# A hybrid encoder layer in float32: weight buffers of the first SwiGLU block, a raw pool, the place of a query projection, and a second bank for side work

## The chip, the cores and the metric

The kernel runs on one core of a Trainium2 chip, in one launch. A core has TensorE (matrix products; PE in the rows, PEld its weight loads), VectorE (DVE), ScalarE (ACT), GpSimd (POOL) and SyncE, whose queue (SP) issues all of this kernel's DMA transfers, in order. The metric is device microseconds of one execution; lower is better.

## The reference

One encoder layer is applied to two requests (1024 and 256 tokens, handled here as 1280 columns), model width 1024, all in float32:

```python
def encoder_layer(x, mem, ...):
    m = mixer(x, ...)              # differential attention | bidirectional RG-LRU, gated, then one projection
    x = layer_norm(ALPHA * x + m, ...)
    x = layer_norm(ALPHA * x + cross_attention(x, mem, ...), ...)   # 4 heads, 256 memory tokens
    x = layer_norm(ALPHA * x + swiglu(x, w_in, w_out), ...)         # 2816 hidden features
...
# in the mixer
proj = x @ w_in                    # q, k, v, x and y of the RG-LRU, two gates
attn_out = diff_attention(q, k, v, lam)     # 8 heads of 2 x 64; softmax - lam * softmax
merged = sigmoid(g_attn) * (attn_out @ p_attn) + sigmoid(g_lru) * (lru_out @ p_lru)
return merged @ w_mix_out
```

## The kernel before

Every float32 product is made of three float32r products: both operands are split into a high part (a copy) and a low part (value minus copy), and high x high, high x low and low x high are added in PSUM. A weight block of 128 x 1024 is loaded as `raw`, copied to `wh` (ScalarE in most stages, L187) and subtracted to `wl` (GpSimd or VectorE, L190) by `wload`. Its result lies in `WT`, four pairs of buffers that live through the whole kernel; `raw` lies in `RW`, two buffers, or in another pool that the caller names.

The stages, in order of time: input projections with the RG-LRU; attention; attention projection and gating (L961 to L963); mixing projection with layer norm; cross-attention; its output projection with layer norm; SwiGLU and the last layer norm, in two halves of 640 tokens.

*Attention.* A unit is a head and 128 query rows. `scores` writes `s` (two buffers of two banks), VectorE reduces (L743), ScalarE takes the exponential (L745), `probs` combines the two halves (L761) and transposes them (`t`, L767), and `values` multiplies (`o`, L785 to L787) and normalises with the tile `pm` (L794, L799). `t` and `pm` share the pool `ps_t`, of two banks. Between units TensorE gets side work from a generator, `fillers`: the memory's keys and values, the gates `sld` and `sad` (evicted with a tanh, L697) and `p_lru` (evicted by L705), each multiplication of 24 matmuls (L283, L286, L287) on the pool `ps_m`, of one bank. The tokens come in three chunks, and the last in the generator's order has columns 512 to 1023. The order of the program is not that of the engines: a scheduler orders each engine's instructions by a priority (the order of the program, and for fillers 120 places later) and by when it thinks that an instruction can start. A pool hands out its buffers in the order of the program, and each waits until the buffer's last holder is done.

*Cross-attention.* For each head `h` and chunk `c` the loop projects queries and then runs the units of the pair before (`prev`), 256 tokens each. `prepare` computes the seven sums of weights of SwiGLU blocks 0 to 3 and stores them in `fpd`.

*SwiGLU.* Each of 22 blocks of 128 hidden features is computed by Strassen's seven products (L355 to L357), each with its own weight of 128 x 512, high and low. `reloaded` fetches those of blocks 0 to 3 from `fpd`, in both halves: two of the seven in the buffers of `RW` (block 0) or in one pair of `WT` (blocks 1 to 3), five in the pool `ws`, whose five pairs each block uses up. `out_group` then multiplies with the output weights `wo` of a group of two blocks (L1202 to L1204), which `wload` puts in `WT`. `pair_ops` prepares the weights of the other blocks on the fly, with raw buffers of `RW` and of `rx`, four buffers.

Of the kernel before, what the change touches and what calls it, by code (L numbers as in the profile page):

```python
# [10 lines left out]
F32R = mybir.dt.float32r  # L11
I32 = mybir.dt.int32
AF = mybir.ActivationFunctionType
ALU = mybir.AluOpType
# [30 lines left out]
RELOAD = 4  # L45
# [83 lines left out]
E_FO = 'VG'  # L129
# [11 lines left out]
def encoder_layer_kernel(ctx: ExitStack, tc: tile.TileContext, i, y_out):  # L141
    nc = tc.nc
    V, S, G, PE, SP = nc.vector, nc.scalar, nc.gpsimd, nc.tensor, nc.sync

    EN = {"V": V, "S": S, "G": G}
# [7 lines left out]
    def f32(ap):  # L153
        return ap.bitcast(F32)
# [110 lines left out]
    WT = pool(ctx, "wt", 4)  # L265
    RW = pool(ctx, "raw", 2)

    def wload(src, heng, leng, wp=WT, rp=RW):
        raw = rp.tile([128, 1024], F32, tag="raw", name="raw")
        SP.dma_start(raw, src)  # L270
        h = wp.tile([128, 1024], F32R, tag="wh", name="wh")
        l = wp.tile([128, 1024], F32R, tag="wl", name="wl")
        split(h, l, raw, heng, leng)
        return h, l

    def gemm_fm(pp, w, op, evac, tag="mm", name="ps", after=None):
        wh, wl = w
        hs, ls, n = op
        ps = pp.tile([128, 512], F32, tag=tag, name=name)[:, :n]
        for k in range(8):  # L280
            a, b = (z[:, k * 128:k * 128 + 128] for z in (wh, wl))
            h, l = hs[k // 2][:, k % 2, :], ls[k // 2][:, k % 2, :]
            ins = PE.matmul(ps, a, h, start=(k == 0), stop=False)  # L283
            if after is not None and k == 0:
                tc.add_manual_dep(ins.ins, after.ins.name, ORDER, reason="order")
            PE.matmul(ps, a, l, start=False, stop=False)  # L286
            PE.matmul(ps, b, h, start=False, stop=(k == 7))  # L287
        evac(ps)
# [370 lines left out]
    with ExitStack() as es:  # L659
# [16 lines left out]
        def fillers():  # L676
            for j in range(16):
                w = wload(i["xa_wkv"][j], EN[E_FWH], EN[E_FWL])
                stage = st.tile([128, M], F32, tag="mst", name="mst", bufs=MSTB)
                gemm_fm(ps_m, w, mem, lambda ps: S.activation(stage, ps, AF.Copy, scale=0.0625 if j < 8 else 1.0), tag="m", after=anchor[0])  # L680
                if j < 8:
                    SP.dma_start(kxd[j], stage)
                else:
                    ps = ps_m.tile([128, 512], F32, tag="m", name="ps")
                    for t in range(4):
                        PE.transpose(ps[:, t * 128:t * 128 + 128], stage[:, t * 128:t * 128 + 128], ident)
                    vt = st.tile([128, 4, 128], F32, tag="mst", name="mvt", bufs=MSTB)
                    S.activation(vt, ps.rearrange("p (t e) -> p t e", e=128), AF.Copy)
                    SP.dma_start(vxd[:, (j - 8) * 128:(j - 7) * 128].rearrange("(t p) e -> p t e", p=128), vt)
                yield 5.3  # L690
            for c0, n in (CHUNKS[2], CHUNKS[0], CHUNKS[1]):
                x = stored(xd, c0, n)
                for dst, base in ((sld, 48), (sad, 40)):
                    for b in range(NB):
                        w = wload(i["w_in"][base + b], EN[E_FWH], EN[E_FWL])
                        g = st.tile([128, M], F32, tag="mst", name="th", bufs=MSTB)[:, :n]
                        gemm_fm(ps_m, w, x, lambda ps: S.activation(g, ps, AF.Tanh, scale=0.5), tag="m", after=anchor[0])  # L697
                        SP.dma_start(dst[b, :, c0:c0 + n], g)
                        yield 5.4 * n / 512
                lru = stored(lrud, c0, n)  # L700
                for b in range(NB):
                    w = wload(i["p_lru"][b], EN[E_FWH], EN[E_FWL])
                    g = st.tile([128, M], F32, tag="mst", name="g", bufs=MSTB)[:, :n]
                    SP.dma_start(g, sld[b, :, c0:c0 + n])
                    gemm_fm(ps_m, w, lru, lambda ps: V.scalar_tensor_tensor(g, g, 1.0, ps, ALU.add, ALU.mult), tag="m", after=anchor[0])  # L705
                    SP.dma_start(gd[b, :, c0:c0 + n], g)
                    yield 5.4 * n / 512

# [266 lines left out]
    with ExitStack() as es:  # L975
# [24 lines left out]
        with ExitStack() as es1:  # L1000
# [100 lines left out]
            prev = None  # L1101
            for h in range(4):
                for c in range(3):
                    now = h, c, queries(h, c)
                    if (h, c) in PREAT:
                        with tc.high_priority(offset=-PREP):
                            prepare(PREAT[h, c])
                    if prev is not None:
                        attends(*prev)
                    prev = now  # L1110
# [5 lines left out]
    with ExitStack() as es:  # L1116
# [44 lines left out]
        with ExitStack() as es1:  # L1161
# [6 lines left out]
            po = pool(es1, "psE", 2, PSUM)  # L1168

            def reloaded(f):  # L1170
                if f == 0:
                    gs = [RW.tile([128, 1024], F32, tag="raw", name="raw").bitcast(F32R) for t in "hl"]
                else:
                    gs = [WT.tile([128, 1024], F32R, tag="w" + t, name="w" + t) for t in "hl"]
                u = [tuple(ws.tile([128, 512], F32R, tag=t, name="s" + t) for t in "hl") for _ in range(5)]
                w = [tuple(g[:, c * 512:c * 512 + 512] for g in gs) for c in range(2)] + u
                for n, _ in P_ORDER:
                    for m in range(2):
                        SP.dma_start(f32(w[n][m]), fpd[f, n, m])
                return w  # L1180
# [30 lines left out]
            for half_ in range(2):  # L1211
                r0 = half_ * 640
                ys = []
                groups = [tuple(range(sum(GR[half_][:n]), sum(GR[half_][:n + 1]))) for n in range(len(GR[half_]))]
                for fs in groups:
                    hs_ = []
                    for f in fs:
                        hs_.append(hidden(f, *((E_M1, E_SL1) if f == NF - 1 else (E_M, E_SL))))
                        if pending:
                            z, t = pending.pop()  # L1220
                            xf = rx.tile([128, 8, 128], F32, tag="raw", name="xf")
                            feature_major(po, "o", z, xf)
                            save(xf, t - 5)
                    if not ys:
                        for t in range(5):
                            ys.append(yp.tile([128, D], F32, tag="z", name="y"))
                            SP.dma_start(ys[t], x2d[r0 + t * 128:r0 + t * 128 + 128, :])
                    wo = [wload(i["ffn_out"][f], EN[E_FO[0]], EN[E_FO[1]]) for f in fs]
                    last = None
                    if fs is groups[-1]:  # L1230
                        SP.dma_start(gt, i["ln3_g"].partition_broadcast(128))
                        SP.dma_start(bt, i["ln3_b"].partition_broadcast(128))
                        if half_ == 0:
                            operands()
                            for j in range(5):
                                xf = rx.tile([128, 8, 128], F32, tag="raw", name="xf")
                                SP.dma_start(xf, x2t[:, :, j * 128:j * 128 + 128].rearrange("k p t -> p k t"))
                                combine(j, xf, rx.tile([128, 4, 4, 64], F32, tag="raw", name="tt"))

                        def last(t):  # L1240
                            rows = slice(r0 + t * 128, r0 + t * 128 + 128)
                            end = half_ == 1 and t == 4
                            with tc.high_priority(offset=0 if half_ else -LNP):
                                power = layer_norm(st, ys[t], gt, bt, end, not (half_ and t >= 3))
                            if end:
                                for hs in (slice(0, 512), slice(512, 1024)):
                                    SP.dma_start(y_out[rows, hs], ys[t][:, hs])
                            if not half_ or t < 3:
                                with tc.high_priority(offset=0 if half_ else -LNP):
                                    G.tensor_tensor(ys[t], ys[t], bt, ALU.add)  # L1250
                            if not end:
                                with tc.high_priority(offset=0 if half_ else -LNP):
                                    SP.dma_start(y_out[rows, :], ys[t])

                    out_group(hs_, fs, wo, ys, fs[0] == 0, last)
# [65 lines left out]
```

## Time and profile before

| | |
|---|---|
| median of 3 runs | 2826.33 us (2823.35 to 2829.81) |
| the profiled execution | 2822.44 us, its span 2820.5 us |
| TensorE busy | 2739.3 us of the span |
| VectorE, ScalarE, GpSimd busy | 1705.5, 1138.6, 919.3 us |

Times in the trace count from the start of the span. A matmul's duration in it is longer than the step to the next one, since they are pipelined; only idle time between them is a wait.

### The profile page before, as it was taken

The page shows a single profiled execution, that of the slowest core. Times are in us where ns is not written, and L with a number is a line of the kernel's source. Part 1 is how long each engine was busy: PE and PEld are TensorE (multiplying, and loading weights), DVE is VectorE, ACT ScalarE, POOL GpSimd, SP SyncE. Part 2 cuts the span into 40 slices and gives each one's busy share as a digit, 9 for nine tenths or more (in the row PEclk, how much of TensorE's full clock was granted, in tenths as well). Part 3 has the DMA queues.
Part 4 walks back from the last instruction along what each step waited for, and adds up shares of the span by engine and source line. Part 5 has one row for each costly group of instructions (what it writes and reads, how often), then busy time and mean ns, then how long its engine had stood idle before and what let it go on. Part 6 is the DMA issues. An engine that isn't in the chain of part 4 may idle for free.

```text
span 2820.5 us, 40319 instructions
## 1 busy us (share of the span) xinstructions
PE 2739.3 (97%) x15240; PEld 2411.8 (86%) x15240; DVE 1705.5 (60%) x2517; ACT 1138.6 (40%) x1921; POOL 919.3 (33%) x576
## 2 busy tenths in 40 slices
PE   9999999999999999999999999998999998999998
PEld 7888888887889888888788889887999997899997
DVE  4545667415667755644345576563677777577776
ACT  3656444415666655455211144321223333233232
POOL 0000000013345543344100100052566559565555
PEclk9999999999999999999999999999999999999999
DMA  9633545565567756844887576658322225622221
GB/s 358 208 109 112 175 152 190 174 206 178 162 202 222 244 169 199 252 141 162 303 273 235 172 276 210 217 186 299 116 79 90 83 82 193 227 84 80 79 80 60
DMA packets 292450, 496.26 MB, mean 176 GB/s; under 512 B 22560, under 2 KB 165664, under 8 KB 292256
## 3 DMA queue, kind: packets, MB, share of 16 engines
q1 hardware_dynamic: 292256, 493.69, 53.6%
q8 instruction: 120, 1.97, 0.3%
q14 instruction: 74, 0.61, 0.1%
HBM read 342.08 MB, written 151.52 MB: 175 GB/s over the span
## 4 chain that ended last, share of the span: by engine, by line
PE 67%; DVE 11%; DMA 11%; issue 4%; ACT 4%; POOL 2%; SPq 1%; DVEq 0%; ACTq 0%; POOLq 0%
PE ps L283 4%; PE ps L286 4%; PE ps L287 4%; PE ps L357 3%; PE ps L355 3%; PE ps L356 3%; PE ps L520 3%; PE ps L521 3%; PE ps L522 3%; PE o L1202 3%; PE o L1203 3%; PE o L1204 2%; PE ps L885 2%; PE ps L883 2%; PE ps L884 2%
## 5 line engine op out<-in xcount | busy, mean ns | idle before, releaser
L190 POOL TENSOR_TENSOR wl<-raw,wh 128x1024 fp32r<-128x1024 f32 x132 | 321.3, 2435 | 973.5 <-ACT wh L187 863.6
L187 ACT ACTIVATE wh<-raw 128x1024 fp32r<-128x1024 f32 (+1 forms) x224 | 224.4, 1006 | 492.0 <-PE ps L286 155.2
L520 PE MATMUL ps<-xh,wh 128*128 128x512 f32 (+1 forms) x768 | 274.4, 357 | 12.1 <-ACT xh L187 5.9
L355 PE MATMUL ps<-xbh,sh 128*128 128x320 f32 x880 | 273.1, 310 | 8.9 <-DMA sh<-fpd 7.0
L521 PE MATMUL ps<-xl,wh 128*128 128x512 f32 (+1 forms) x768 | 273.9, 357 | 0.5 <-DVE xl L190 0.5
L357 PE MATMUL ps<-xbh,sl 128*128 128x320 f32 x880 | 272.6, 310 | 0.4 <-DMA sl<-fpd 0.3
L522 PE MATMUL ps<-xh,wl 128*128 128x512 f32 (+1 forms) x768 | 273.0, 356 | 0.0
L356 PE MATMUL ps<-xbl,sh 128*128 128x320 f32 x880 | 272.4, 310 | 0.0
L283 PE MATMUL ps<-fh,wh 128*128 128x512 f32 (+1 forms) x704 | 258.6, 367 | 11.7 <-DVE g L705 5.0
L286 PE MATMUL ps<-fl,wh 128*128 128x512 f32 (+1 forms) x704 | 255.7, 363 | 2.5 <-DMA fl<-memd 2.5
L287 PE MATMUL ps<-fh,wl 128*128 128x512 f32 (+1 forms) x704 | 255.1, 362 | 0.0
L190 DVE TENSOR_TENSOR wl<-raw,wh 128x1024 fp32r<-128x1024 f32 (+1 forms) x136 | 177.5, 1311 | 96.6 <-ACT wh L187 84.7
L743 DVE TENSOR_REDUCE nm<-s 128x1 f32<-128x1024 f32 (+1 forms) x160 | 167.3, 1059 | 93.8 <-PE s L742 93.4
L1205 DVE SCALAR_TENSOR_TENSOR y<-y,o 128x512 f32<-128x512 f32 x200 | 133.5, 681 | 115.4 <-PE o L1204 108.0
L850 POOL TENSOR_TENSOR rstd<-rstd,mhalf 128x1 f32<-128x1 f32 x30 | 34.5, 1152 | 498.4 <-DVE rstd L849 498.4
L1202 PE MATMUL o<-wh,hh 128*128 128x512 f32 x440 | 175.0, 398 | 11.8 <-DVE wh L189 4.3
L745 ACT ACTIVATE e<-s,nm 128x1024 f32<-128x1024 f32 (+1 forms) x160 | 158.6, 996 | 57.6 <-DVE nm L743 55.7
L355 PEld LDWEIGHTS ps<-xbh,sh 128*128 128x128 f32 x880 | 165.8, 188 | 12.8 <-DMA sh<-fpd 8.4
L520 PEld LDWEIGHTS ps<-xh,wh 128*128 128x128 f32 x768 | 146.3, 190 | 34.3 <-ACT xh L187 5.9
L1203 PE MATMUL o<-wl,hh 128*128 128x512 f32 x440 | 173.1, 394 | 0.0
L356 PEld LDWEIGHTS ps<-xbl,sh 128*128 128x128 f32 x880 | 165.9, 189 | 3.8
L357 PEld LDWEIGHTS ps<-xbh,sl 128*128 128x128 f32 x880 | 165.7, 188 | 3.4 <-DMA sl<-fpd 0.9
(261 smaller groups left out, 7241.6 us busy)
## 6 DMA issues: line engine op xcount, KB each, us to landing
raw<-w_in SPq DMA_DIRECT2D x80, 512.0 KB
raw<-ffn_in SPq DMA_DIRECT2D x80, 512.0 KB
raw<-ffn_out SPq DMA_DIRECT2D x44, 512.0 KB
q<-qd SPq DMA_DIRECT2D x320, 64.0 KB
raw<-p_lru SPq DMA_DIRECT2D x24, 512.0 KB
qd<-hl SPq DMA_DIRECT2D x16, 640.0 KB
kd<-hl SPq DMA_DIRECT2D x16, 640.0 KB
vd<-v SPq DMA_DIRECT2D x40, 256.0 KB
```

The source lines that it names most:

```text
L190: leng.tensor_tensor(l, src, f32(h), ALU.subtract)
L283: ins = PE.matmul(ps, a, h, start=(k == 0), stop=False)
L286: PE.matmul(ps, a, l, start=False, stop=False)
L287: PE.matmul(ps, b, h, start=False, stop=(k == 7))
L355: PE.matmul(ps, w[n][0][:, ks], xb[m][0][:, k, :], start=(k == 0), stop=False)
L356: PE.matmul(ps, w[n][0][:, ks], xb[m][1][:, k, :], start=False, stop=False)
L357: PE.matmul(ps, w[n][1][:, ks], xb[m][0][:, k, :], start=False, stop=(k == 3))
L520: PE.matmul(ps, wh[:, ks], h[:, k, :], start=(k == 0), stop=False)
L521: PE.matmul(ps, wh[:, ks], l[:, k, :], start=False, stop=False)
L522: PE.matmul(ps, wl[:, ks], h[:, k, :], start=False, stop=(k == 7))
L1202: PE.matmul(ps, hs_[a][0][:, ts], wo[a][0][:, hs], start=(a == 0), stop=False)
L1203: PE.matmul(ps, hs_[a][0][:, ts], wo[a][1][:, hs], start=False, stop=False)
```

## The change

Four edits. In the last chunk the p_lru multiplications of odd `b` take their bank from `ps_t`, the others from `ps_m` as before. In the cross-attention the last query projection, of (3, 2), is written behind the units of (3, 1). In the first half SwiGLU block 0 takes all seven weights from the four pairs of `WT`, and block 1 takes the two buffers of `RW`; the second half is as before. The output weights of blocks 0 to 3 are loaded through `rx` in place of `RW`.

```diff
                     w = wload(i["p_lru"][b], EN[E_FWH], EN[E_FWL])
...
-                    gemm_fm(ps_m, w, lru, lambda ps: V.scalar_tensor_tensor(g, g, 1.0, ps, ALU.add, ALU.mult), tag="m", after=anchor[0])
+                    last = c0 == 512 and b % 2
+                    gemm_fm(ps_t if last else ps_m, w, lru, lambda ps: V.scalar_tensor_tensor(g, g, 1.0, ps, ALU.add, ALU.mult), tag="t" if last else "m", after=anchor[0])
...
             for h in range(4):
                 for c in range(3):
+                    if (h, c) == (3, 2):
+                        attends(*prev)
+                        prev = None
                     now = h, c, queries(h, c)
...
             def reloaded(f):
-                if f == 0:
+                if f == 0 and not half_:
+                    z = [[WT.tile([128, 1024], F32R, tag="w" + t, name="w" + t) for t in "hl"] for _ in range(4)]
+                    w = [tuple(y[:, c:c + 512] for y in x) for x in z for c in (0, 512)][:7]
+                    for n, _ in P_ORDER:
+                        for m in range(2):
+                            SP.dma_start(f32(w[n][m]), fpd[f, n, m])
+                    return w
+                if f == 1 - half_:
                     gs = [RW.tile([128, 1024], F32, tag="raw", name="raw").bitcast(F32R) for t in "hl"]
...
-                    wo = [wload(i["ffn_out"][f], EN[E_FO[0]], EN[E_FO[1]]) for f in fs]
+                    wo = [wload(i["ffn_out"][f], EN[E_FO[0]], EN[E_FO[1]], rp=rx if f < RELOAD else RW) for f in fs]
```

What it makes of the order of the engines is shown at three places. Line numbers are those of each kernel (in the changed one they are one higher from L706 on, and up to eleven higher at the end).

The first is ScalarE where TensorE comes to the last chunk's first gates: `th` is the eviction of a filler, `wh` the copy of a filler's weight, `e` the exponential, `pth` and `pf` the copies of a transposition, `sq` and `ob` the end of a pair; the numbers tell the tiles apart. Before:

```order
L187 ACTIVATE wh_10600<-raw_10598 128x1024
L745 ACTIVATE e_12249,ss_12234<-s_12243,nm_12233 128x1024
L697 ACTIVATE th_10228<-ps_10229 128x512
L770 ACTIVATE pth_11904<-t_12018 128x4x128
L773 ACTIVATE pf_12024<-t_12018 128x512
L745 ACTIVATE e_12241,ss_12234<-s_12235,nm_12233 128x1024
L770 ACTIVATE pth_12125<-t_12135 128x4x128
L187 ACTIVATE wh_10731<-raw_10729 128x1024
L697 ACTIVATE th_10359<-ps_10360 128x512
L770 ACTIVATE pth_12127<-t_12142 128x4x128
```

And with the change:

```order
L790 ACTIVATE sq_12180<-o_12155 128x256
L792 ACTIVATE ob_12182<-o_12155,g08_84 128x256
L187 ACTIVATE wh_10600<-raw_10598 128x1024
L697 ACTIVATE th_10228<-ps_10229 128x512
L187 ACTIVATE wh_10731<-raw_10729 128x1024
L697 ACTIVATE th_10359<-ps_10360 128x512
L187 ACTIVATE wh_10810<-raw_10808 128x1024
L697 ACTIVATE th_10393<-ps_10394 128x512
L187 ACTIVATE wh_10923<-raw_10921 128x1024
L697 ACTIVATE th_10570<-ps_10571 128x512
```

Such pairs of a copy and an eviction follow each other 14 times, with nothing of the attention between; on TensorE 325 matmuls of fillers stand in one run there.

The second is TensorE where the attention ends and the attention projection (`ps<-fh,wh`, L961 before, L962 now) begins. Before, fillers stand between the last rows of the attention, and after these come 120 more matmuls of fillers (five multiplications) and then the projection:

```order
L794 MATMUL pm<-ones,sq 128x1 x2
L799 MATMUL pm<-ident,rs 128x128 x2
L283 MATMUL ps<-fh,wh 128x512
L286 MATMUL ps<-fl,wh 128x512
L287 MATMUL ps<-fh,wl 128x512
```

With the change the last filler stands 308 matmuls ahead of the projection, and all of these are the attention's; the last are:

```order
L768 MATMUL t<-ident,e 128x128 x2
L800 MATMUL pm<-ident,rs 128x128 x2
L795 MATMUL pm<-ones,sq 128x1 x2
L786 MATMUL o<-pth,vh 128x256
L787 MATMUL o<-ptl,vh 128x256
L788 MATMUL o<-pth,vl 128x256
...
L800 MATMUL pm<-ident,rs 128x128 x2
L795 MATMUL pm<-ones,sq 128x1 x2
L800 MATMUL pm<-ident,rs 128x128 x2
L962 MATMUL ps<-fh,wh 128x512 x8
```

The projection also begins with the first product of all eight blocks, where it began with one block.

The third is the queue SP between the halves of SwiGLU: `ffn_out` is an output weight, `y<-y` an output of the first half, `wh`, `wl`, `sh`, `sl` the reloaded weights of a block. Before:

```order
L327 DMA raw<-ffn_in 128x1024
L1253 DMA y<-y 128x1024
L1227 DMA y<-x2d 128x1024
L1179 DMA wl<-fpd 128x512
L1179 DMA wh<-fpd 128x512 x2
L1179 DMA wl<-fpd 128x512
L1253 DMA y<-y 128x1024 x2
L1179 DMA sh<-fpd 128x512
L1179 DMA sl<-fpd 128x512
L1231 DMA lng<-ln_g 128x1024
L1227 DMA y<-x2d 128x1024
L270 DMA raw<-ffn_out 128x1024 x2
```

And with the change:

```order
L270 DMA raw<-ffn_out 128x1024 x3
L1264 DMA y<-y 128x1024
L270 DMA raw<-ffn_out 128x1024
L1238 DMA y<-x2d 128x1024
L1264 DMA y<-y 128x1024
L1190 DMA wh<-fpd 128x512
L1190 DMA wl<-fpd 128x512
L1190 DMA wh<-fpd 128x512
```

The four output weights of blocks 0 to 3 stand ahead of the outputs and of the reloaded weights now; two of them stood behind three outputs.

## Rows read from the trace of the kernel before

**Rows 1.** The page's part 1: busy time, share of the span, instructions.

```profile
PE 2739.3 (97%) x15240; PEld 2411.8 (86%) x15240; DVE 1705.5 (60%) x2517; ACT 1138.6 (40%) x1921; POOL 919.3 (33%) x576
```

**Rows 2.** Windows: length, busy per engine (instructions), granted TensorE clock, DMA share, GB/s.

```profile
1193.60:1393.90 200.30, 193.23 (x1016) 162.99 (x1016) 95.75 (x150) 94.36 (x173) 71.32 (x43) 0.99 0.58 193
1781.40:1813.40 32.00, 25.40 (x190) 24.11 (x189) 23.20 (x41) 18.46 (x41) 0.00 (x0) 0.91 0.94 315
1807.30:1814.30 7.00, 4.88 (x22) 4.40 (x21) 3.37 (x4) 2.12 (x4) 0.00 (x0) 0.52 1.16 330
1929.70:1957.00 27.30, 18.81 (x117) 17.67 (x116) 10.78 (x19) 5.70 (x9) 3.24 (x3) 0.87 0.96 343
1937.00:1944.00 7.00, 2.80 (x10) 2.80 (x11) 0.69 (x1) 0.51 (x1) 0.00 (x0) 0.52 0.95 343
2370.00:2417.00 47.00, 37.42 (x220) 33.94 (x218) 23.74 (x37) 8.38 (x11) 29.56 (x17) 0.93 0.87 319
2394.50:2401.50 7.00, 4.94 (x15) 4.07 (x16) 4.04 (x4) 0.00 (x0) 5.45 (x3) 0.51 1.04 413
1387.50:1391.00 3.50, 3.50 (x10) 2.76 (x9) 1.17 (x1) 0.72 (x1) 0.00 (x0) 0.53 0.83 270
```

**Rows 3.** Waits of TensorE, 1184 to 1394: total us, times, longest.

```profile
PE ps L283 <- DVE g L705: 4.5, 5, 2.1
```

**Rows 4.** Timeline near the side work's end: start, duration, [idle before <-releaser].

```profile
1376.47 0.39 PE L283 MATMUL ps<-fh,wh 128*128 128x512 f32 x1
...
1377.15 0.39 PE L283 MATMUL ps<-fh,wh 128*128 128x512 f32 x1
...
1384.77 1.22 DVE L190 TENSOR_TENSOR wl<-raw,wh 128x1024 fp32r<-128x1024 f32 x1 [2.10 <-ACT wh L187]
1385.91 0.68 DVE L705 SCALAR_TENSOR_TENSOR g<-g,ps 128x512 f32<-128x512 f32 x1
...
1386.74 0.47 PE L283 MATMUL ps<-fh,wh 128*128 128x512 f32 x1 [2.15 <-DVE g L705]
```

**Rows 5.** Waits of TensorE, 1781 to 1960.

```profile
PE ps L355 <- DMA sh<-fpd: 5.8, 1, 5.8
PE o L1068 <- DVE ob L190: 5.3, 3, 2.1
PE t L932 <- DVE z L858: 1.4, 1, 1.4
...
PE s L1045 <- ACT e L1053: 1.1, 1, 1.1
```

**Rows 6.** Waits of TensorE, 2368 to 2420.

```profile
PE o L1202 <- DVE wh L189: 4.3, 1, 4.3
```

**Rows 7.** Groups by line and shape, ScalarE, 1140 to 1340: count, busy, mean ns.

```profile
L187 ACT ACTIVATE wh<-raw 128x1024 fp32r<-128x1024 f32 x22 | 23.3, 1059 | 69.1 <-PE ps L286 47.7 <-issue 13.6 <-DMA raw<-p_lru 5.1
...
L697 ACT ACTIVATE th<-ps 128x512 f32<-128x512 f32 x16 | 9.3, 580 | 0.0
```

**Rows 8.** Timeline of ScalarE: one copy of a filler's weight.

```profile
1134.68 1.06 ACT L187 ACTIVATE wh<-raw 128x1024 fp32r<-128x1024 f32 x1 [4.30 <-PE ps L286]
```

**Rows 9.** Groups by line and shape, VectorE, 1140 to 1340.

```profile
L743 DVE TENSOR_REDUCE nm<-s 128x1 f32<-128x1024 f32 x30 | 36.3, 1219 | 26.6 <-PE s L742 26.6
L761 DVE SCALAR_TENSOR_TENSOR e<-e,r 128x1024 f32<-128x1024 f32 x16 | 21.3, 1328 | 0.5
L776 DVE TENSOR_TENSOR ptl<-t,pth 128x512 fp32r<-128x512 f32 x16 | 11.0, 685 | 3.1 <-ACT pth L770 3.1
L760 DVE SCALAR_TENSOR_TENSOR s1q<-ss 128x1 f32<-128x1 f32 x20 | 8.9, 443 | 3.6 <-ACT e L745 3.4
L759 DVE SCALAR_TENSOR_TENSOR r<-ss,nlam,r 128x1 f32<-128x1 f32 x20 | 7.6, 382 | 2.6 <-ACT e L745 2.0
```

## The prediction

> **What bounds the kernel now.** The page's first part is read first: TensorE is busy for 2739.3 us, 97% of the span [rows 1]. Its work is the same before and after (15162 instructions of TensorE stand in either order), so an edit can only win or lose what TensorE idles, and what it computes at the lower clock. The windows by stage say where that is, and the change touches four such places [rows 2].
>
> - End of the attention, 1193.6 to 1393.9: busy 193.2 of 200.3 us, so 7.1 us idle. Most of it lies at the very end, where only side work is left: five waits for L705, 4.5 us together [rows 3]. One gap ends 0.83 us after L705 starts, which itself stands behind a weight split on VectorE [rows 4]. After the longest (2.15 us) the granted clock is 0.53 for 3.5 us, that is 1.2 GHz: about 1.7 us lost.
> - End of the cross-attention, 1781.4 to 1813.4: 25.4 of 32.0 us busy, 6.6 idle. Then 0.52 granted for 7 us, about 3.4 lost. The waits are those of L1068 and L1045 [rows 5].
> - Start of the first SwiGLU block, 1929.7 to 1957.0: 18.8 of 27.3 us busy, 8.5 idle, the longest wait 5.8 us for the loads of `sh` from `fpd` [rows 5]. The clock falls while it waits, and 2.8 us of work run at 0.52: 1.4 lost.
> - Start of the second half's SwiGLU, 2370 to 2417: 37.4 of 47.0 us busy, 9.6 idle, 4.3 of it for `wh` of an output weight [rows 6]. Then 0.51 granted, with 4.9 us busy: 2.4 lost.
>
> **Part by part: where it wins.**
>
> *The first block's weights in the four weight buffers.* They come free when the output projection has used rows 4 to 7 of its weight for the last time, 48 matmuls into its last 96. In the order of the queue SP all 14 loads now stand in one piece where four stood, ahead of the stores of the last two token tiles. The other 48 matmuls take 48 x 0.227 = 11 us (three take 0.68 [rows 4]), so the loads have that long before their first use. The 8.5 us of idle time and the 1.4 us of slow clock should go; I take 9 of 9.9 (bounds 5 and 9.9).
>
> *Last query projection behind its units.* 26 of its 48 matmuls still fill the gap before the units of (3, 1); the other 22 now stand among them, and 30 matmuls of the next projection stand between the last units. They need `oh` of the first token tile, which is stored and loaded back through memory, and TensorE may wait there. I take 7.5 of the 6.6 + 3.4 us (bounds 4 and 10).
>
> *Output weights by the other raw pool.* In the second half `raw` holds the reloaded weights of block 0, and `ffn_out` had to queue behind them. Its four loads now stand ahead of the last outputs. The 4.3 us and the slow 2.4 us go; but the DMA engines are busy for 0.87 of that stretch at 319 GB/s [rows 2], and the next weights may be late instead. I take 5 (bounds 0 and 10).
>
> Together 21.5 us won, bounds 9 and 30.
>
> **Part by part: where it loses.** The filler of odd `b` in the last chunk now takes a buffer of `ps_t`. That pool has two, and every later transposition (`t`) and normalisation (`pm`) of the attention needs one in turn. Buffers are handed out in the order of the program, but the fillers run some 14 multiplications behind it, since their priority is lower. So the first of the four (`b` = 1) holds its place in the rotation, and the attention behind it waits until all the older fillers have run. The order shows it: from about 1194 us of this trace, TensorE has 325 filler matmuls in a row, 13.5 multiplications of 24, with not one of the attention between them; and after the last filler come 308 matmuls of the attention alone. Three terms follow.
>
> *The run of fillers.* Until the chunk's eighth p_lru everything is still on the one bank of `ps_m`. Each multiplication waits until the last one is evicted, and nothing covers it. The eviction is a tanh of 0.58 us on ScalarE, and the new order puts a weight split of 1.06 us right in front of each [rows 7]. That split can't start earlier: with four weight buffers it overwrites the operand of the multiplication that just ends, as its present wait on L286 shows [rows 8]. L286 is the second last matmul, 0.23 us before the end (three matmuls take 0.68 us [rows 4]). So the gap is 1.06 + 0.58 - 0.23 and some 0.3 for semaphores, 1.7 us. Its bounds are the gaps of today's end: 0.6 on the mean of the four short ones (4.5 us less the one of 2.1, over four [rows 3]) and the 2.15 of the one with a split in front of its eviction; I take 1.7, since a split stands in front of each. 13.5 x 1.7 = 23 us, bounds 8 and 29.
>
> *The stretch with both.* 239 filler matmuls with some attention between, 12 changes of bank: 3 us (bounds 0 and 8).
>
> *The attention alone.* TensorE's 308 matmuls are 56 of 512 columns at 0.68 / 3 = 0.227 us, 140 of 256 at half that, and 112 smaller ones, at most as long: some 41 us. VectorE has in that stretch 14 reductions of 1024 columns at 1.219 (17.1), 8 sums at 1.328 (10.6), 9 low parts at 0.685 (6.2), 20 scalars at 0.38 to 0.44 (8.2) [rows 9], 8 weight splits of the coming `p_attn` at 1.22 (9.8 [rows 4]), which now stand in it instead of under the fillers, and 43 smaller ones, by an estimate of a third of a microsecond each 14.5: 66 us. VectorE bounds it, so TensorE idles 66 - 41 = 25, and 2 more until the last unit's normalisation is through: 27 us. Bounds: 12 (VectorE a fifth faster than its rows, with GpSimd quiet) and 45 (see the second rival).
>
> Against this the 7.1 + 1.7 us of the old end are gone. Loss: 23 + 3 + 27 - 8.8 = 44 us, bounds 11 and 73.
>
> **Sum.** 44 - 21.5 = 22.5 us more. The profiled execution has 2822.4 us for a span of 2820.5, and is 3.9 under the median of the runs, 2826.3; 2822.4 + 22.5 = 2845, and on the median 2849. I say 2848.
>
> One rule of the Trainium skill speaks for the change. The row shows the same gap again and again on TensorE, at each change of the single bank [rows 3]. The Trainium skill (Perfetto Trace Analysis, Optimization Strategy) says that consistent bubbles, the same gap repeating on the engine that should be saturated, can mean that there isn't enough SBUF or PSUM for the next tile. By that rule a second bank wins the 8.8 us, and the time would be 2826 - 8.8 - 21.5 = 2796. The same section also says that stretches with different most-contended engines may gain from being interleaved; here VectorE's stretch and TensorE's are pulled apart. By the rows and the order, the second holds, and it is 2848.
>
> **Rivals.**
>
> 1. *The order is reshuffled and nothing is lost* (faster). What was put off must be done anyway, and if the other engines keep up, TensorE stays busy in the run and in the tail. For it: equal work, and VectorE is busy for only 95.8 of the 200.3 us [rows 2]. Against it: in the run VectorE has nothing to do, since `s` has two buffers and no unit can go ahead, and what it leaves undone comes back in one piece. Time: down to 2826.3 - 8.8 - 21.5 = 2796; it decides where the added idle time is under 25 us, against my 53.
> 2. *The clock falls in the tail* (slower still). TensorE would idle two fifths of it, and after waits of such a share the three stages above were granted 0.51 to 0.53. At 1.2 GHz its 41 us become 82, over VectorE's 66, so some 15 us more: 2863. For it: those rows. Against it: there the idle time was in pieces of 2 us and more, here it is spread.
> 3. *The wins are given back.* The second half is bound by loads and the cross-attention waits for `oh`; only the first block's 9 us stay: 2860.
> 4. *The pieces cancel*, with the run's gap at 0.6 (8 us), 3 us between, 15 in the tail: 26 - 8.8 - 21.5 is 4 us less, so within 0.2%, 2821 to 2832.
>
> **How the numbers follow.** My forecast (2834 to 2857) has 0.45, rival 1 0.1, rival 2 0.2, rival 3 0.15, rival 4 0.1. The range takes in the forecast, rivals 2 and 3 with a few us beyond, and half of rival 4: 2826 to 2867. What the measurement can tell from no change is 0.2%, 5.6 us: faster 0.1, same 0.1, slower 0.8.
>
> **What the profile after would show.** Right: a stretch of some 95 us from 1194 us on with hardly any `s`, `t` or `o` on TensorE and a wait on `th` of 1.5 to 1.9 us at each of 13 places; some 65 to 80 us without a filler before the attention projection, with VectorE the busiest engine; no wait of 5 us on `sh` at the first SwiGLU block; no wait on `wh` at L1202 in the second half. Wrong: gaps of 0.9 us or less in that run, or a tail of 45 us with TensorE at 90%; then the loss is half of mine. A projection that starts no later than 1394 us would refute it all.

## The result and the profile after

The changed kernel takes 2868.45 us (median of 5 runs, 2861.1 to 2874.91), against 2826.33 before (2823.35 to 2830.09): 1.0148 times as long, 95% interval 1.0134 to 1.0161, or 42 us more. Forecast were 2848 and the range 2826 to 2867. The direction was right and the end of the attention cost what was forecast; the 21.5 us that the three other edits were to win came to a fifth of that. One of the twelve runs of the first block alone (below) took 7007 us and is left out of its ratio as a slow run.

The profiled execution has 2874.9 us, 6.5 above the median. It reaches the end of the attention already 6.8 us late (the 408th `t` starts at 1158.50 us where it started at 1151.66), in a part whose order is the same; the profile of the second bank alone (below) has 0.4 us there. The stages below are therefore compared by how much each adds.

The page's part 1 answers to [rows 1]:

```profile
PE 2762.0 (96%) x15240; PEld 2421.7 (84%) x15240; DVE 1692.7 (59%) x2517; ACT 1140.2 (40%) x1921; POOL 913.5 (32%) x576
```

The span is 2873.1 us. Idle time of TensorE grew from 81 to 111 us. Its busy time grew by 23 us with the same instructions. It was busy for 53.7 us at a granted 0.50 (1.2 GHz), where before it was for 22.8; half of the added 31 us, some 15, is lost to the lower clock. The rest is by estimate the ends of matmuls in front of gaps: the run's 325 matmuls of fillers, 73.9 us at 0.227 each, are 77.9 us busy at a granted 1.00.

Windows of the kernel after (columns as in [rows 2]): the run of fillers, the stretch with both, the attention alone, and the first 10.5 us of the attention projection; then two pieces of the third.

```profile
1201.20:1299.90 98.70, 78.20 (x327) 59.87 (x326) 1.22 (x1) 21.57 (x29) 31.11 (x14) 1.00 0.38 121
1299.90:1373.30 73.40, 73.01 (x374) 61.08 (x374) 28.40 (x48) 25.59 (x49) 25.04 (x15) 1.00 0.59 199
1373.30:1441.50 68.20, 52.63 (x326) 43.60 (x324) 59.10 (x103) 49.77 (x100) 18.56 (x17) 0.91 0.46 140
1441.50:1452.00 10.50, 9.64 (x25) 7.16 (x26) 2.68 (x4) 1.47 (x2) 0.00 (x0) 0.59 1.01 361
...
1385.00:1400.00 15.00, 13.00 (x80) 10.35 (x78) 15.00 (x22) 11.29 (x23) 4.63 (x4) 1.00 0.58 165
1400.00:1415.00 15.00, 11.79 (x74) 9.50 (x73) 14.97 (x27) 12.10 (x24) 3.99 (x4) 1.00 0.06 19
```

In the run TensorE is idle for 20.5 us and VectorE does 1.2 us of work in 99. Its 325 matmuls follow each other as the order said. In the tail VectorE is busy without a break from 1385 to 1415, and TensorE has idle time beside it.

One gap of the run, in the timeline (rows of the weight loads left out):

```profile
1247.55 0.39 PE L286 MATMUL ps<-fl,wh 128*128 128x512 f32 x1
1247.78 0.39 PE L287 MATMUL ps<-fh,wl 128*128 128x512 f32 x1
1248.03 1.06 ACT L187 ACTIVATE wh<-raw 128x1024 fp32r<-128x1024 f32 x1 [5.64 <-issue]
1248.99 0.58 ACT L697 ACTIVATE th<-ps 128x512 f32<-128x512 f32 x1
...
1249.62 0.50 PE L283 MATMUL ps<-fh,wh 128*128 128x512 f32 x1 [1.45 <-ACT th L697]
```

The copy starts at 1248.03, 0.1 us after the last L286 has ended (1247.55 + 0.39): it needs the buffer that L286 reads. The profile itself names no releaser for it. The eviction stands behind that copy, and TensorE behind the eviction. The waits of TensorE in the run, 1201 to 1300, where [rows 3] had 4.5 us in five:

```profile
PE ps L283 <- ACT th L697: 19.2, 13, 1.7
```

The chain of work through the end of the tail, up to the projection's eighth product:

```profile
1416.21 0.83 DVE r L760
1417.11 1.25 DVE e L762
1418.36 0.60 DVE ptl L777
...
1431.84 3.79 DMA raw<-p_attn
1435.65 1.07 ACT wh L187
1436.74 0.59 DVE wl L190
...
1437.99 6.59 DMA raw<-p_attn
1444.61 1.06 ACT wh L187
1445.71 0.79 PE ps L962
```

Up to about 1420 us VectorE leads. From there to 1431.7 VectorE, GpSimd and TensorE alternate in the chain, TensorE in part at the lower clock. After that, to 1444.6, two loads of `p_attn` lead: six of the projection's eight weights are loaded after 1422 us, one behind the other, through the two buffers of `RW`. The projection begins with the first product of all eight blocks. Seven of these stand from 1441.57 on, when their first `fh` has landed, and the eighth waits for the last weight until 1445.71.

The three other places answer to [rows 5, 6]. Waits of TensorE at the end of the cross-attention, 1833 to 1880, then on to 2020:

```profile
PE ps L884 <- DMA oh<-otd: 1.9, 1, 1.9
PE o L1069 <- DVE ob L190: 0.6, 1, 0.6
```

```profile
PE ps L884 <- DMA oh<-otd: 2.9, 1, 2.9
PE o L1213 <- ACT hh L187: 2.7, 1, 2.7
PE ps L886 <- DMA ol<-otd: 0.5, 1, 0.5
```

And at the start of the second half, 2415 to 2475:

```profile
PE ps L355 <- DMA sh<-fpd: 4.8, 2, 4.4
PE ps L355 <- ACT sg L149: 3.1, 1, 3.1
PE o L1215 <- POOL hl L190: 0.7, 2, 0.4
```

Of the waits that the edits aimed at (5.3 us on `ob`, 5.8 on `sh` in the first block, 4.3 on `wh`) 0.6 us on `ob` are left, and at each place another stands: `oh` twice, `hh`, and `sh` again. The distance of the two traces, taken at the same matmuls, grows by 45.6 us from that `t` to the projection's 72nd first product and by 3.7 over the end of the cross-attention and the start of its output projection; it falls by some 6 at the first block and by 0.6 at the second half's start.

### The profile page after: what moved, and what is told of

It is laid out like the page before. It is cut to its first block, busy times and chain, and to the rows that moved or that the text cites. A ratio compares the mean times of both kernels' runs of the same rounds, so it can differ in the third digit from the quotient of the medians.

```text
span 2873.1 us, 40312 instructions
## 1 busy us (share of the span) xinstructions
PE 2762.0 (96%) x15240; PEld 2421.7 (84%) x15240; DVE 1692.7 (59%) x2517; ACT 1140.2 (40%) x1921; POOL 913.5 (32%) x576
## 3 DMA queue, kind: packets, MB, share of 16 engines
q1 hardware_dynamic: 292256, 493.69, 52.6%
## 4 chain that ended last, share of the span: by engine, by line
PE 37%; DVE 6%; DMA 6%; POOL 3%; issue 2%; ACT 1%; SPq 0%; DVEq 0%; POOLq 0%; ACTq 0%
PE ps L357 3%; PE ps L356 3%; PE ps L355 3%; PE o L1213 3%; PE o L1215 2%; PE o L1214 2%; PE ps L886 2%; PE ps L884 2%; DMA raw<-ffn_in 2%; PE ps L885 2%; PE ps L963 1%; PE ps L1034 1%; PE ps L1035 1%; PE ps L964 1%; PE ps L1036 1%
## 5 line engine op out<-in xcount | busy, mean ns | idle before, releaser
L355 PE MATMUL ps<-xbh,sh 128*128 128x320 f32 x860 | 266.7, 310 | 7.9 <-DMA sh<-fpd 4.8
L357 PE MATMUL ps<-xbh,sl 128*128 128x320 f32 x860 | 266.6, 310 | 0.0
L356 PE MATMUL ps<-xbl,sh 128*128 128x320 f32 x860 | 266.4, 310 | 0.0
L286 PE MATMUL ps<-fl,wh 128*128 128x512 f32 (+1 forms) x704 | 255.5, 363 | 3.3 <-DMA fl<-memd 2.4
L283 PEld LDWEIGHTS ps<-fh,wh 128*128 128x128 f32 x704 | 132.7, 189 | 55.0 <-ACT th L697 26.6
L1215 PE MATMUL o<-wh,hl 128*128 128x512 f32 x440 | 169.1, 392 | 0.9 <-POOL hl L190 0.9
```

The costliest lines, as they stand in the source:

```text
L355: PE.matmul(ps, w[n][0][:, ks], xb[m][0][:, k, :], start=(k == 0), stop=False)
L356: PE.matmul(ps, w[n][0][:, ks], xb[m][1][:, k, :], start=False, stop=False)
L357: PE.matmul(ps, w[n][1][:, ks], xb[m][0][:, k, :], start=False, stop=(k == 3))
```

## The experiments

Each was timed in five rounds against the kernel before, 4 to 12 runs a kernel; the ratio stands with its 95% interval, and us are the ratio's share of 2826.

**The second bank alone.** The first hunk of the change and nothing else.

```diff
+                    last = c0 == 512 and b % 2
+                    gemm_fm(ps_t if last else ps_m, w, lru, lambda ps: V.scalar_tensor_tensor(g, g, 1.0, ps, ALU.add, ALU.mult), tag="t" if last else "m", after=anchor[0])
```

> Only the second bank for odd b of the last chunk. Theory (the loss is the whole of this edit and lies at the end of the attention; the profile of the changed kernel lost 45.6 us there): 2826 + 45 = 2871, a run of 325 matmuls of fillers with some 20 us idle, and no filler in the last 65 us of the attention. Rival (the other three edits lose some 20 us of the 42 by new waits, and this one is worth only half): 2826 + 22 = 2848.

Measured: 2873.29 us, 1.0160 (1.0144 to 1.0177), 45 us more. The whole loss is this edit's.

**The other three.** The change without that hunk.

```diff
-                    last = c0 == 512 and b % 2
+                    gemm_fm(ps_m, w, lru, lambda ps: V.scalar_tensor_tensor(g, g, 1.0, ps, ALU.add, ALU.mult), tag="m", after=anchor[0])
```

> The three other edits without the second bank. Theory (the stages of the changed kernel read as they stand: 3.7 us lost at the cross-attention's end, 5.8 won at the first SwiGLU block, 0.6 at the second half's start): 2826 - 3 = 2823, with waits of 2 to 3 us on oh at two places. Rival (the 21.5 us that were forecast are there, and in the changed kernel the lower clock and the shifted order hid them): 2826 - 21.5 = 2805.

Measured: 2820.53 us, 0.9983 (0.9972 to 0.9994): 4.8 us won. The forecast wins are nowhere hidden; they are not there.

**The query projection alone.**

```diff
+                    if (h, c) == (3, 2):
+                        attends(*prev)
+                        prev = None
```

> Only the last query projection behind the units of (3, 1). Theory (the wait is moved, not removed: oh is stored and read back, and the first two token tiles of the output projection now end together): 2826 + 4 = 2830, with a wait of 2.9 us on oh for the third tile. Rival (the gap of 10 us is filled): 2819.

Measured: 2830.43 us, 1.0013 (1.0002 to 1.0023), 4 us slower. Its waits, 1780 to 1900:

```profile
PE ps L883 <- DMA oh<-otd: 5.4, 2, 3.1
PE o L1068 <- DVE ob L190: 0.6, 1, 0.6
```

**The first block alone.**

```diff
+                if f == 0 and not half_:
+                    z = [[WT.tile([128, 1024], F32R, tag="w" + t, name="w" + t) for t in "hl"] for _ in range(4)]
...
-                if f == 0:
+                if f == 1 - half_:
```

> Only the first SwiGLU block in the four weight buffers. Theory (as in the changed kernel): 2826 - 6 = 2820, no wait on sh at the start of the block, but one of 2.7 us on hh behind it. Rival 1 (all of the 9 us forecast): 2817. Rival 2 (the loads only come late elsewhere, nothing is won): 2826.

Measured: 2824.84 us, 0.9989 (0.9977 to 1.0001): 3 us less, not told from no change. Its waits, 1931 to 2046:

```profile
PE o L1209 <- DVE wh L189: 2.2, 1, 2.2
PE o L1210 <- POOL wl L190: 2.0, 2, 1.7
PE o L1209 <- ACT hh L187: 1.7, 2, 1.1
```

The wait on `sh` is gone, and 4.2 us on the output weights are new: block 1 now holds the two buffers of `RW` that they are loaded through.

**One filler on the pool.** One p_lru in place of four takes a bank of `ps_t`.

```diff
-                    last = c0 == 512 and b % 2
+                    last = c0 == 512 and b == 7
```

> As the second bank alone, but only the last p_lru (b = 7) takes a buffer of ps_t, one filler in place of four. Theory (the loss comes from the place that the filler holds in the pool's rotation, not from the count of banks lent): one is enough; the order has a run of 361 filler matmuls and 274 of the attention alone at the end, so 15 x 1.5 + some 20 us: 2826 + 40 = 2866. Rival (each lent bank costs its share, a quarter of 46): 2838.

Measured: 2875.31 us, 1.0169 (1.0154 to 1.0184), 48 us more: as much as four. What costs is the place in the rotation, not the number of banks lent.

**Held, then two banks.** The generator stops ahead of the last chunk's p_lru and goes on when the attention's last unit is written.

```diff
                 lru = stored(lrud, c0, n)
+                if c0 == 512:
+                    held[0] = filled[0]
+                    yield 0.0
...
-                while filled[0] < upto:
+                while filled[0] < min(upto, held[0]):
...
+        held[0] = 1e9
         fill(1e9)
```

> The last chunk's p_lru fillers are written behind the last unit of the attention, so that no later t or pm follows them in the rotation; odd b takes ps_t as in the change. The order of the attention stays that of before. Theory: the waits on the single bank at the end go (4.5 us) and the slow clock behind them (1.7): 2826 - 6 = 2820. Rival 1 (a pool that is shared with the attention costs whatever the place): 2860 or more. Rival 2 (the weight splits bound that stretch, the bank was not the limit): 2826.

Measured: 2819.43 us, 0.9968 (0.9955 to 0.9981), 9 us won. The waits on the bank are gone; of 1184 to 1400 there remain, beside two of 0.3 us and less,

```profile
PE ps L283 <- DMA fh<-lrud: 0.9, 1, 0.9
PE ps L286 <- DMA fl<-xd: 0.3, 1, 0.3
```

**The output weights alone.**

```diff
+                    wo = [wload(i["ffn_out"][f], EN[E_FO[0]], EN[E_FO[1]], rp=rx if f < RELOAD else RW) for f in fs]
```

> Only the output weights of blocks 0 to 3 through rx. Theory (the second half's start is bound by its loads; the wait on wh goes and comes back on sh): 1 us, 2825. Rival (the 5 us forecast): 2821.

Measured: 2826.95 us, 1.0000 (0.9991 to 1.0009). Alone it wins nothing.

**First block and output weights together**, both hunks above.

```diff
+                if f == 0 and not half_:
...
+                    wo = [wload(i["ffn_out"][f], EN[E_FO[0]], EN[E_FO[1]], rp=rx if f < RELOAD else RW) for f in fs]
```

> First block in the four weight buffers, and output weights through rx. Theory (the first needs the second: alone its output weights waited behind the raw buffers that block 1 now holds, 4 us on wh and wl): together 4.5 in the first half and 1.5 in the second, 2826 - 6 = 2820. Rival (the two are independent: 1 us of the one, 1 of the other): 2824.

Measured: 2818.37 us, 0.9966 (0.9954 to 0.9978), 10 us. Together they win, apart they gave 3 and 0: the second clears the queue that the first makes. The waits on `wh` and `wl` are gone from the first half; of 1927 to 2050 there remain

```profile
PE o L1209 <- ACT hh L187: 3.9, 1, 3.9
PE o L1209 <- DVE y L1212: 0.6, 1, 0.6
```

**Held, one bank** (control).

```diff
-                    last = c0 == 512 and b % 2
+                    last = False
```

> Control for the held fillers: the last chunk's p_lru written behind the last unit, but all on the single bank of ps_m. Theory (the 9 us that holding and a second bank won are the bank's): 2826, with the waits of TensorE on the bank at the end as before. Rival (they come from writing the fillers later): 2819.

Measured: 2830.18 us, 0.9998 (0.9986 to 1.0010). Holding alone changes nothing, so the 9 us are the bank's. Waits at the end, 1184 to 1402:

```profile
PE ps L283 <- DVE g L708: 6.8, 5, 2.2
```

**The query projection and three buffers.**

```diff
-            ot = pool(es1, "ot", 2)
+            ot = pool(es1, "ot", 3)
```

> The last query projection behind its units, and three buffers in place of two for oh and ol of the output projection. Theory (its loss is the third token tile: the first two end together, their two buffers come free together, and a load of 3 us lies open): that wait and the slow clock behind it go, some 4 us, 2830 - 4 = 2826. Rival (the loss is in the units themselves): 2830, with the wait gone and no gain.

Measured: 2825.86 us, 0.9989 (0.9980 to 0.9998), against 1.0013 with two buffers: 7 us better. The wait on `oh` of the first tile is left, 2.5 us, where with two buffers 5.4 stood for the first and the third. Issues of `oh` for the third and the fourth tile on SP, in the kernel before:

```profile
1825.75 0.36 SPq L1139 DMA_DIRECT2D oh<-otd  x1
1835.72 0.36 SPq L1139 DMA_DIRECT2D oh<-otd  x1
```

with the query projection moved and two buffers:

```profile
1833.26 0.36 SPq L1142 DMA_DIRECT2D oh<-otd  x1
1834.34 1.26 SPq L1142 DMA_DIRECT2D oh<-otd  x1
```

and with three:

```profile
1817.44 0.37 SPq L1142 DMA_DIRECT2D oh<-otd  x1
1828.76 0.36 SPq L1142 DMA_DIRECT2D oh<-otd  x1
```

Before, the two loads are 10 us apart; with the edit 1.1 us, so both buffers come free together; with the third buffer the third tile's load goes out 22.8 us after the first tile's, where it was 34.0.

**Held fillers on two banks, with both weight edits.**

```diff
+                    held[0] = filled[0]
...
+                if f == 0 and not half_:
...
+                    wo = [wload(i["ffn_out"][f], EN[E_FO[0]], EN[E_FO[1]], rp=rx if f < RELOAD else RW) for f in fs]
```

> Held fillers on two banks, first block in the four weight buffers, output weights through rx; the query projection as before. Theory (two places, nothing shared): 2826 - 9 - 9 = 2808. Rival (the lower clock takes part of it back, as each stage then starts at another moment): 2813.

Measured: 2811.15 us, 0.9938 (0.9922 to 0.9955), 17.5 us faster: about the sum of the two (9 and 10), and faster than either kernel.

**All four, mended**: the same with the query projection behind its units and `ot` of three.

```diff
+                        attends(*prev)
...
+            ot = pool(es1, "ot", 3)
```

> As the one before, with the query projection behind its units and three buffers for oh and ol. Theory (the edit of the query projection is mended by the third buffer and then wins part of its 10 us): 2804. Rival (it stays neutral at best): 2808 or more.

Measured: 2807.6 us, 0.9924 (0.9905 to 0.9943), 21.5 us faster than before and some 60 faster than the change. Its interval overlaps that of the version above, so the last step is not shown by the times; what it does at its place stands at the end of this section.

**No residual in the second half.**

```diff
-                            SP.dma_start(ys[t], x2d[r0 + t * 128:r0 + t * 128 + 128, :])
+                            if not half_:
+                                SP.dma_start(ys[t], x2d[r0 + t * 128:r0 + t * 128 + 128, :])
...
+                        if first and half_:
+                            V.tensor_scalar(ys[t][:, hs], ps, 1.0, None, ALU.mult)
```

> First block in the four weight buffers and output weights through rx, and in the second half the five token tiles of the residual are neither loaded nor added (its output lacks ALPHA times x there). That takes 2.5 MB out of the start of the second half, 6 us at the 400 GB/s of that stretch. Theory (the 5 us forecast for the output weights went into loads: the wait on wh became one on sh, behind the same full DMA engines): 2818 - 5 = 2813, the wait on sh there mostly gone. Rival (the stretch is bound by the arithmetic of VectorE and GpSimd, both busy there): 2818.

This is the first block and the output weights together, and the kernel leaves out the residual of the second half, ALPHA times x.

Measured: 2821.48 us, 0.9984 (0.9976 to 0.9992), against 0.9966 with the residual: no gain. My theory of the loads falls. The waits, 2360 to 2480:

```profile
PE o L1209 <- ACT hh L187: 4.7, 1, 4.7
PE ps L355 <- ACT sg L149: 2.8, 1, 2.8
```

The wait on `sh` is gone, and `hh` holds TensorE instead.

**Splits off VectorE**, on the second bank alone.

```diff
-        ws = [wload(i["p_attn"][b], S, V, wte if b < 4 else WT) for b in range(8)]
+        ws = [wload(i["p_attn"][b], S, G, wte if b < 4 else WT) for b in range(8)]
```

> The second bank alone, with the weight splits of p_attn on GpSimd in place of VectorE. Theory (in the tail without fillers VectorE is the bound, 59 of 68 us, of these 9 for seven such splits): the tail is shorter by 9 us, 2873 - 9 = 2864. Rival (GpSimd takes 2.4 us for a split and the normalisation's rs then waits behind it): 2873 or more.

Measured: 2873.25 us, 1.0169 (1.0154 to 1.0185), nothing won. GpSimd's rs is not it: TensorE waits for it 7.0 us here, 7.3 without the edit. In the second bank's trace the eight splits stand from 1416 to 1440 us, the last six each behind a load through `RW`; the piece that VectorE fills is ahead of them. My theory had them at the wrong place. The run doesn't say what bounds those last 20 us: on GpSimd a split takes 2.4 us in place of 1.2, its raw buffer is held longer, and the last of six loads goes out at 1447.7 where it went out at 1432.0.

**Copies off ScalarE**, on the second bank alone.

```diff
-                        w = wload(i["w_in"][base + b], EN[E_FWH], EN[E_FWL])
+                        w = wload(i["w_in"][base + b], V if c0 == 512 else EN[E_FWH], EN[E_FWL])
```

> The second bank alone, with the copies wh of the last chunk's gate weights on VectorE, idle in that run, in place of ScalarE. Theory (each of the 13 gaps of 1.46 us is a copy of 1.06 and a tanh of 0.58, less the overlap; without the copy the tanh starts when the last matmul ends): gaps of 0.65 us, 13 x 0.8 = 10.5 us less, 2873 - 10.5 = 2862. Rival (the next matmul waits for the copy itself wherever it is): 2873.

Measured: 2857.8 us, 1.0112 (1.0097 to 1.0127), 14 us better than the second bank alone. TensorE's waits on `th` fell from 19.5 to 10.4 us, and the stretch from the last filler to the projection from 68.4 to 65.1; why the latter is shorter was not tested. Two gaps of its run, in the timeline:

```profile
1237.94 0.50 PE L283 MATMUL ps<-fh,wh 128*128 128x512 f32 x1 [0.74 <-ACT th L697]
...
1244.43 0.50 PE L283 MATMUL ps<-fh,wh 128*128 128x512 f32 x1 [0.74 <-ACT th L697]
```

Half of each gap was the copy in front of the eviction; the other half is the tanh itself, which a single bank can't hide.

**At the places themselves.** How much longer (+) or shorter (-) a stretch of the trace before is in the other traces, in us, taken at the same matmuls:

| stretch | nothing in it edited | edited |
|---|---|---|
| 1780 to 1900, end of the cross-attention | -0.1 to +0.3 (11 traces) | query projection +2.2 to +3.7 (3); with three buffers -3.6 and -3.8 |
| 1900 to 2340, first half of SwiGLU | -0.4 to +4.0 (8) | first block alone +0.5; output weights alone +3.3; both -1.6 to -6.2 (6) |
| 2340 to 2500, second half's start | -0.6 to +2.8 (8) | output weights -0.1 to -1.4 (6) |

So the loss of the query projection and its mending are clear of the noise of single traces, and so is the win of the two weight edits together. The 3.3 us of the output weights alone and the 1 us in the second half are not.

## Why the prediction was right and wrong

**The place of the fillers: right.** That a late filler's place in `ps_t` holds up the attention is shown by one filler that costs as much as four, and by the held fillers, which use the same banks and win. "44 us, bounds 11 and 73" came to 45.6 in the trace and 45 alone.

**Its parts.** The run: 23 forecast, 20.5 idle measured, 13 gaps of 1.46 (1.7 forecast), the copy shown to be half of each. The stretch with both: 3 forecast, 0.4 measured. The tail: 27 forecast; 68.2 us less 41 of work at the full clock are 27.2, 15.6 of them idle. Not forecast: the projection starts at a granted clock of 0.59 and loses some 5 us more (25 matmuls, 5.7 us at 0.227 each, fill 10.5), and its last weight is late.

**The tail's mechanism was only half right.** "VectorE bounds it", 66 us: it was busy for 59.1, without a break between 1385 and 1415, but it led the chain only to about 1420, and from 1431.8 on the loads of `p_attn` did. That these loads bound the end is read from the chain; no run tests it. Rival 2, the clock, came true in small part: TensorE was granted 0.50 from 1422.9 to 1429.7 and again from 1436.6 on, and did 7.7 us of its busy time in the tail there, so some 4 us were lost. What else lies between the 41 us of work and the 52.6 busy is by estimate the ends of matmuls in front of gaps. The departures cancel, so the term is right by more luck than the working shows.

**The working.** Both pages count 15240 instructions of TensorE, not 15162, and the tail has 324, 128 of them small, not 308 and 112; that adds at most 2 us to the 41. At the end of the cross-attention the 3.4 us count idle time twice: of the 7 us at 0.52 only 4.9 were busy, 2.3 us lost, so the place was worth 8.9 and not 10.

**The wins: wrong, and this is the step that failed.** "Together 21.5 us won, bounds 9 and 30" is 4.8 us, under the lower bound. Term by term:

- "I take 7.5" for the query projection: it costs 4. I had named the wait on `oh` of the first tile, and bounded the term at 4 won; the row that was missing is the third tile. Both buffers of the first two tiles now come free together, and the next load lies open (3.1 us of wait alone, 2.9 in the changed kernel). Three buffers turn the loss into a gain of 3.
- "I take 9 of 9.9" for the first block: some 6 in the changed kernel, and alone 3 us that can't be told from nothing (0.9989, interval to 1.0001). I priced it as independent. It takes the raw buffers of block 1, and needs the other edit to pay. What is left of the gap waits on `hh`, 2.7 us where 1.3 stood.
- "I take 5" for the output weights: 0 alone, 0.6 at its place, within the noise of a trace. "The next weights may be late instead" was written down, and that is what the trace shows; but taking 2.5 MB of loads away does not help either, since `hh` then takes over. Which of the chains behind `hh` (VectorE, GpSimd, the lower clock) sets that stretch stays open.

Rival 3, "the wins are given back", at 2860 with a chance of 0.15, was the case that came; with nothing for the first block either it would have read 2870. Its reason for the second half, a stretch bound by loads, is not borne out by the kernel without the residual.

**The rule.** The single bank's repeated gap is real. The Trainium skill (Perfetto Trace Analysis, Optimization Strategy) says that such bubbles can mean too little SBUF or PSUM for the next tile. The held fillers agree: a second bank won them 9 us, where the prediction had 8.8 from its rows. It holds for the bank, not for this way of getting it.

## What to carry to other kernels

A buffer taken from another stage's pool takes a place in that pool's rotation, and the rotation follows the order of the program: if the work that takes it has a lower priority, everything after it waits for that work. Write the borrower behind the pool's last user, and the same bank wins. A wait's length is not what its removal wins. Three waits of 5.3, 5.8 and 4.3 us gave 4.8 together, since another wait ended close behind each; the bank's 4.5 gave 9, with the shorter idle pieces and the slow clock around them. Look for the second wait that ends within a few us of the first, and price edits that share a buffer (here `RW`) together.

## What the runs showed of the hardware that was not expected

The clock did not fall in the run of fillers, where TensorE idled 20.5 of 98.7 us in gaps of about 1.5 us: 1.00 was granted throughout. In the tail it did. From 1385 to 1415 us TensorE was busy for 24.8 of 30 us at 1.00; then for 5.1 of 7.9 us, and in a gap of 2.7 us the granted clock fell, to 0.50 from 1422.9 on:

```profile
1415.00:1422.90 7.90, 5.14 (x43) 4.90 (x43) 7.72 (x16) 6.73 (x18) 3.88 (x3) 1.00 0.11 35
1422.90:1429.70 6.80, 5.32 (x23) 4.63 (x24) 5.05 (x9) 3.46 (x8) 2.00 (x2) 0.50 0.65 193
1436.60:1441.50 4.90, 2.33 (x10) 1.45 (x8) 2.57 (x5) 2.33 (x5) 0.69 (x1) 0.50 0.88 293
```

In the trace of the second bank alone, in the same piece of the tail, it fell without such a gap, after 10 us with 7.6 busy and 1.3 us as the longest gap:

```profile
1399.00:1409.00 10.00, 7.64 (x50) 5.94 (x49) 10.00 (x18) 7.90 (x17) 2.26 (x4) 1.00 0.07 21
1409.00:1412.40 3.40, 3.40 (x18) 3.40 (x18) 3.30 (x7) 1.42 (x5) 1.29 (x1) 0.50 0.18 58
```

What made the difference between the two traces stays open.
